# Reciprocal roots of RMS norms: a power on GpSimd with an addition on VectorE, in place of Ln and Exp on ScalarE

## The chip, the cores and the metric

The kernel runs on all eight cores of one Trainium2 chip. Each core computes one of the eight samples of the batch, and no core waits for another. The metric is the device time of the slowest core, in microseconds (us). Executions of a kernel mostly agree within a few tenths of a per cent, but some fall into a slower state, in which the four cores of one die show a lower granted TensorE clock and the time is longer by some per cent, whatever the kernel. Such runs are called slow below.

## The reference

The model is a trunk of two layers. Each layer has three sub-layers (a SwiGLU feed-forward block, a mixer, a second feed-forward block), and each sub-layer begins with an RMS norm over 1024 channels. A last norm follows, so there are seven norms over 2048 tokens. The code is shortened.

```python
D_MODEL = 1024; BATCH = 8; SEQ = 2048; EPS = 1e-6

def rmsnorm(x, g):
    y = x * lax.rsqrt(jnp.mean(x * x, axis=-1, keepdims=True) + EPS)
    return y * g

def modulate(x, g, mod):
    shift, scale, gate = jnp.split(mod, 3, axis=-1)
    return rmsnorm(x, g) * (1.0 + scale) + shift, gate

# per layer:  x += 1/2 * gate * SwiGLU_1(h);  x += gate * Mixer(h);  x += 1/2 * gate * SwiGLU_2(h)
#             with h, gate = modulate(x, ...) before each;  at the end: rmsnorm(x, final_g)
```

The change concerns one thing alone: how `rsqrt(mean + EPS)` is computed.

## The kernel before

Activations lie transposed. `X` has the 128 channels of a chunk in the partitions, eight chunks, and 2048 tokens along the free dimension, worked on in four tiles of `TT = 512` tokens. The sum of squares over channels therefore runs across partitions, and TensorE forms it: ScalarE squares the chunks, and eight matmuls with a 128x128 matrix of ones add them. Every one of the 128 rows of the result in PSUM (a 128x512 tile) holds the same sum, so it can be multiplied into `X` as it is. ScalarE turns it into the reciprocal root as exp(-0.5 ln(x)), and VectorE multiplies.

```python
def ones_pair(t, c, b):                       # sum over channels, broadcast to all partitions
    for x in (c, c + 1):
        n = 12 * (t // 2) + x
        add("pe", I("matmul", PS[b][:], ONES[:], TB[:, n, :].bitcast(BF16), start=(x == 0), stop=(x == NC - 1)), ...)

def rstd_ops(ts, bs):                         # the part that changes
    for t, b in zip(ts, bs):
        rs, k = rs_of(t)
        add("act", I("activation", out=rs, in_=PS[b][:], func=AF.Ln, scale=1.0 / D, bias=EPSB[:, 0:1]),
            reads=[("ps", b), "EPSB"], writes=k)
        BK.give(b)
    for t in ts:
        rs, k = rs_of(t)
        add("act", I("activation", out=rs, in_=rs, func=AF.Exp, scale=-0.5), reads=k, writes=k)

# in apply_units: the multiply that waits for rs
add("dve", I("tensor_tensor", out=role.hbuf[:, c:c + 2, tsl(t)], in0=X[:, c:c + 2, tsl(t)],
             in1=rs.unsqueeze(1).broadcast_to([128, 2, TT]), op=ALU.mult), ...)
# ... (cut)
```

`add(engine, instruction, reads, writes)` appends to a list per engine. Each engine executes its list in order and waits at an instruction until what it reads and writes is free. So an instruction that waits holds up all later ones of its engine. GpSimd, otherwise nearly idle, issues the DMAs that load the weights and convert them from fp32 to fp16 (`SLIN<-wp`, `SLOUT<-wp` in the profile), in the same in-order list. And the program has 24 places with a 128x512 reciprocal root: six stages (the prologue, the entry of the first mixer, the second feed-forward block, the second layer's first block, the stage of the pooling mixer, and the final norm), each with four token tiles. Two more, of 128x8, belong to the pooling mixer.

## Time and profile before

The median was 2119.45 us of three runs (2114.96 to 2266.61; the run of 2266.61 us was slow).

| before | value |
|---|---|
| time, median | 2119.45 us |
| span of the profiled slowest core (core 2) | 2134.3 us |
| TensorE (PE) busy | 95% |
| VectorE (DVE) / ScalarE (ACT) / GpSimd (POOL) busy | 64% / 33% / 5% |
| mean granted clock per core | 0.971 to 0.989 |

In this profiled execution cores 2 and 3 were mildly slowed (clock 0.971 and 0.972, spans 2134.3 and 2132.5 us); the other six took 2104.6 to 2111.5 us.

Lines from the page of the kernel before: busy time of each engine with its share of the span and its instructions, then the busy tenths in 40 equal slices of the span (9 is 90% or more), then the chain of waits that ended last by engine.

```profile
PE 2037.6 (95%) x9611; PEld 918.9 (43%) x9634; DVE 1361.1 (64%) x2573; ACT 709.9 (33%) x1068; POOL 117.1 (5%) x227
...
PE   6999999999999989999998899999998899999996
...
POOL 0000000001210000000000000100100100000000
PEclk9888999999999999999999999999999999999998
...
PE 82%; DVE 8%; issue 4%; ACT 3%; DMA 3%; DVEq 0%; SPq 0%; ACTq 0%; POOL 0%; POOLq 0%
```

The kernel is bound by TensorE from end to end. Nothing that only makes ScalarE faster can win more than TensorE's idle 5%.

Groups of instructions of the kernel before on ScalarE, the five that the change removes or thins out. The columns are line, engine, operation, names, shapes and count, then busy us and mean ns of one, then the engine's idle time just before and what ended it. All lines read L253 because one helper records every instruction.

```profile
L253 ACT ACT_TABLE_LOAD x38 | 48.8, 1283 | 52.0 <-PE ps L253 48.0 <-DMA SM<-small 3.6
...
L253 ACT ACTIVATE TSUM<-ps,EPSB 128x512 f32<-128x512 f32 x20 | 13.5, 687 | 6.7 <-PE ps L253 6.6
...
L253 ACT ACTIVATE TSUM<-TSUM 128x512 f32<-128x512 f32 x20 | 12.1, 627 | 1.1
...
L253 ACT ACTIVATE TP<-ps,EPSB 128x512 f32<-128x512 f32 x4 | 2.7, 687 | 0.0
L253 ACT ACTIVATE TP<-TP 128x512 f32<-128x512 f32 x4 | 2.5, 630 | 0.4
```

`ps,EPSB` are the Ln, the two groups without EPSB the Exp: 30.8 us in all. The table loads come from alternating Ln and Exp with the activations of the blocks. The Trainium skill, ScalarE: Activation LUTs, section "What ACT_TABLE_LOAD costs", gives about 1283 ns for the load, and this trace has 1283.

The only powers in the kernel before, from the same view for GpSimd:

```profile
L253 POOL TENSOR_TENSOR STAT<-STAT,MHALF 128x1 f32<-128x1 f32 x16 | 9.4, 590 | 2.4
```

They have one column each.

Longest waits of TensorE on other engines in the kernel before, with the wait of GpSimd's weight loads for a free slot above them (columns: total us, times, longest us):

```profile
POOL SLIN L253 <- PE ps L253: 1156.5, 91, 64.5
...
PE ps L253 <- DVE ps L253: 23.8, 17, 3.1
...
PE ps L253 <- DVE TSUM L253: 13.4, 7, 7.8
...
PE ps L253 <- ACT TSUM L253: 9.4, 10, 2.7
```

TensorE hardly waits. GpSimd waits most of the time, chiefly for a weight slot that TensorE has to finish with first. It loads ahead by a few slots and no further.

### The profile page before, as it was taken

How to read it: one execution, taken by the hardware profiler on the slowest of the kernel's cores; microseconds unless marked ns; L12 is line 12 of the kernel's file. 1: busy time of each engine (PE TensorE's matmuls, PEld its weight loads, DVE VectorE, ACT ScalarE, POOL GpSimd, SP SyncE). 2: the span in 40 equal slices, each digit the busy share in tenths (PEclk: the TensorE clock that was granted, in tenths of full speed). 3: DMA queues.
4: the chain of work that ended last, by engine and by line, in shares of the span. 5: the costliest groups of instructions: out<-in, count | busy, mean ns of one | idle time of the engine just before them, and what ended most of it. 6: DMA issues, size and time to landing. Idle time of an engine off the chain costs nothing.

```text
span 2134.3 us, 29994 instructions; the slowest of 8 cores (2104.6 to 2134.3 us)
## 1 busy us (share of the span) xinstructions
PE 2037.6 (95%) x9611; PEld 918.9 (43%) x9634; DVE 1361.1 (64%) x2573; ACT 709.9 (33%) x1068; POOL 117.1 (5%) x227
## 2 busy tenths in 40 slices
PE   6999999999999989999998899999998899999996
PEld 1344444444644434444443344444454444444442
DVE  1556677747777777677665876555657675555555
ACT  2531131334422453032125531230354653240342
POOL 0000000001210000000000000100100100000000
PEclk9888999999999999999999999999999999999998
DMA  9535283515046125355352253230543414231313
GB/s 272 143 65 119 90 167 105 127 27 100 10 99 142 27 50 133 93 139 142 98 109 41 46 113 99 45 67 13 90 77 51 80 31 70 39 70 20 65 47 116
DMA packets 73575, 183.45 MB, mean 86 GB/s; under 512 B 7248, under 2 KB 11472, under 8 KB 72528
## 3 DMA queue, kind: packets, MB, share of 16 engines
q0 software_dynamic: 28416, 92.29, 25.4%
q1 hardware_dynamic: 45008, 89.27, 12.8%
q8 instruction: 81, 1.33, 0.3%
q14 instruction: 70, 0.57, 0.1%
HBM read 257.02 MB, written 8.39 MB: 124 GB/s over the span
## 4 chain that ended last, share of the span: by engine, by line
PE 82%; DVE 8%; issue 4%; ACT 3%; DMA 3%; DVEq 0%; SPq 0%; ACTq 0%; POOL 0%; POOLq 0%
PE ps L253 82%; DVE H L253 2%; DVE TP L253 2%; DVE X L253 2%; DMA ACTB<-wm 1%; DMA SLIN<-wp 1%; ACT TP L253 1%; DVE ACTB L253 1%; ACT TSUM L253 1%; DVE TSUM L253 1%; ACT L253 1%; DVE ps L253 1%; DVE WMOD L253 1%; DMA WMOD<-wmod 1%; DVE SLIN L253 0%
## 5 line engine op out<-in xcount | busy, mean ns | idle before, releaser
L253 PE MATMUL ps<-H,SLIN 128*128 128x512 f16 x2240 | 544.9, 386 | 20.8 <-DVE ps L253 15.7
L253 PE MATMUL ps<-TSUM,SLIN 128*128 128x512 f16 x2016 | 506.0, 383 | 22.8 <-DVE TSUM L253 10.7
L253 PE MATMUL ps<-ACTB,SLOUT 128*128 128x512 f16 x2368 | 524.5, 382 | 0.0
L253 DVE SCALAR_TENSOR_TENSOR X<-ps,GH,X 128x512 f32<-128x512 f32 x448 | 332.7, 749 | 235.3 <-PE ps L253 233.9
L253 ACT ACTIVATE TP<-ps 128x512 f32<-128x512 f32 x568 | 336.2, 596 | 387.0 <-PE ps L253 313.5
L253 PEld LDWEIGHTS ps<-ACTB,SLOUT 128*128 128x128 f16 x2368 | 232.7, 98 | 283.7 <-issue 20.9
L253 PEld LDWEIGHTS ps<-H,SLIN 128*128 128x128 f16 x2240 | 219.2, 99 | 296.5 <-issue 63.3
L253 ACT ACTIVATE ps<-ps 128x512 f32<-128x512 f32 x168 | 97.8, 582 | 733.0 <-PE ps L253 670.4
L253 PEld LDWEIGHTS ps<-TSUM,SLIN 128*128 128x128 f16 x2016 | 194.1, 98 | 270.0 <-issue 62.4
L253 PE MATMUL ps<-H,SLOUT 128*128 128x512 f16 x1216 | 280.3, 391 | 1.9 <-DVE H L253 1.6
L253 PEld LDWEIGHTS ps<-H,SLOUT 128*128 128x128 f16 x1216 | 121.2, 100 | 155.5 <-issue 41.2
L253 PE MATMUL ps<-ACTB,SLIN 128*128 128x512 f16 x704 | 171.8, 383 | 8.1 <-DVE ps L253 8.1
L253 DVE TENSOR_TENSOR ACTB<-TP 128x512 f16<-128x512 f32 x140 | 96.8, 691 | 116.5 <-ACT TP L253 113.9
L253 DVE TENSOR_TENSOR ACTB<-TP,ps 128x512 f16<-128x512 f32 x156 | 106.9, 687 | 96.2 <-PE ps L253 90.8
L253 DVE TENSOR_TENSOR SLIN<-SLIN 128x512 f16<-128x512 f16 x404 | 162.3, 418 | 4.3 <-DMA SLIN<-wp 4.2
L253 DVE SCALAR_TENSOR_TENSOR WMOD<-WMOD,CB 128x512 f32<-128x512 f32 x240 | 162.5, 682 | 1.4 <-DMA WMOD<-wmod 1.2
L253 DVE TENSOR_TENSOR ps<-ps,TP 128x512 f32<-128x512 f32 x168 | 117.3, 698 | 59.0 <-PE ps L253 55.0
L253 DVE TENSOR_TENSOR TP<-ps,TP 128x512 f32<-128x512 f32 x168 | 115.6, 688 | 39.4 <-PE ps L253 39.2
L253 POOL DMA_DIRECT2D SLIN<-wp x107 | 57.3, 536 | 1245.3 <-PE ps L253 1156.5
L253 ACT ACTIVATE TSUM<-X 128x1024 bf16<-128x1024 f32 (+1 forms) x88 | 95.8, 1127 | 70.6 <-DVE X L253 44.4
L253 PEld LDWEIGHTS ps<-ACTB,SLIN 128*128 128x128 f16 x704 | 67.9, 98 | 88.8 <-issue 13.3
L253 DVE TENSOR_TENSOR H<-TP 128x512 f16<-128x512 f32 x44 | 30.5, 692 | 59.3 <-ACT TP L253 59.0
(95 smaller groups left out, 841.6 us busy)
## 6 DMA issues: line engine op xcount, KB each, us to landing
WMOD<-wmod SPq DMA_DIRECT2D x240, 256.0 KB, 3.3
SLIN<-wp POOLq DMA_DIRECT2D x107, 512.0 KB, 6.0
SLOUT<-wp POOLq DMA_DIRECT2D x60, 512.0 KB, 9.1
X<-xT SPq DMA_DIRECT2D x8, 1024.0 KB, 33.0
outT<-X SPq DMA_DIRECT2D x16, 512.0 KB, 3.1
H<-wm SPq DMA_DIRECT2D x4, 1024.0 KB, 11.7
H<-X POOLq DMA_DIRECT2D x8, 512.0 KB, 4.6
ACTB<-wm SPq DMA_DIRECT2D x3, 1024.0 KB, 23.7
```

Source lines behind the costliest of these rows:

```text
L253: return lambda E: getattr(E, name)(*a, **k)
```

## The change

The intent is to take work and table loads off ScalarE, and to use GpSimd, which was 5% busy. VectorE adds epsilon while it reads the sum from PSUM, since, as the Trainium skill says in Trainium Kernel Development and Optimization, section "Key Constraints", GpSimd cannot access PSUM. GpSimd then raises the tile to the power -0.5. The division by 1024 moves into the matrix of ones.

```diff
+    def pool_rstd(out, ps, rd, wr, n):
+        add("dve", I("tensor_scalar", out=out, in0=ps, scalar1=EPS, scalar2=None, op0=ALU.add), reads=rd, writes=wr)
+        add("pool", I("tensor_tensor", out=out, in0=out, in1=MHALF[:, 0:1].broadcast_to([128, n]), op=ALU.pow),
+            reads=["MHALF"] + wr, writes=wr)
+
     def rstd_ops(ts, bs):
         for t, b in zip(ts, bs):
             rs, k = rs_of(t)
-            add("act", I("activation", out=rs, in_=PS[b][:], func=AF.Ln, scale=1.0 / D, bias=EPSB[:, 0:1]),
-                reads=[("ps", b), "EPSB"], writes=k)
+            pool_rstd(rs, PS[b][:], [("ps", b)], k, TT)
             BK.give(b)
-        for t in ts:
-            rs, k = rs_of(t)
-            add("act", I("activation", out=rs, in_=rs, func=AF.Exp, scale=-0.5), reads=k, writes=k)
# ... (the same in the prologue, st_rstd, and for the two 128x8 tiles of the pooling mixer)
-    add("dve", I("memset", ONES[:], 1.0), writes=["ONES"])
+    add("dve", I("memset", ONES[:], 1.0 / D), writes=["ONES"])
```

More of the change, by code (lines that the diff above doesn't have):

```diff
@@ L1267, in pool_units @@
         R = STAT[:, p, 0:8]
-        V = STAT[:, p, 8:16]
-        add("act", I("activation", out=V, in_=PS[b][:, 0:8], func=AF.Ln, scale=1.0 / D, bias=EPSB[:, 0:1]),
-            reads=[("ps", b), "EPSB"], writes=[("ST", p, 0), ("ST", p, 1), ("ST", p, 2), ("ST", p, 3)])
-        add("act", I("activation", out=R, in_=V, func=AF.Exp, scale=-0.5), reads=[("ST", p, 0)], writes=[("R", p)])
+        pool_rstd(R, PS[b][:, 0:8], [("ps", b)], [("ST", p, 0), ("ST", p, 1), ("ST", p, 2), ("ST", p, 3), ("R", p)], 8)
         BK.give(b)
@@ L1462, in st_rstd @@
         rs = 4 + t % 2
-        add("act", I("activation", out=TP[:, rs, 0:TT], in_=PS[b][:], func=AF.Ln, scale=1.0 / D, bias=EPSB[:, 0:1]),
-            reads=[("ps", b), "EPSB"], writes=[("TP", rs)])
-        add("act", I("activation", out=TP[:, rs, 0:TT], in_=TP[:, rs, 0:TT], func=AF.Exp, scale=-0.5),
-            reads=[("TP", rs)], writes=[("TP", rs)])
+        pool_rstd(TP[:, rs, 0:TT], PS[b][:], [("ps", b)], [("TP", rs)], TT)
         return rs
```

## The prediction

> **What bounds the kernel.** The page gives PE 2037.6 us busy of 2134.3 (95%), VectorE 64%, ScalarE 33%, GpSimd 5%; the chain of waits is 82% PE. Only about 97 us of PE idleness can be won, some 30 of them before the first weights land. Ln and Exp matter only where a norm's scale is waited for.
>
> **What goes.** By the groups of instructions: 24 Ln (687 ns) and 24 Exp (about 630 ns) on 128x512, two small pairs, and most of the 38 table loads (1283 ns each), since Ln/Exp alternate with Silu and Gelu: about 75 us of ScalarE, which has much idle time. On the chain, table loads are 0.6% (13 us), and waits around Ln and Exp about as much. Ceiling of the gain: 20 to 25 us.
>
> **What comes.** 24 VectorE adds out of PSUM (estimate 0.6 us each, between the 546 ns of a 128x512 fp32 tensor_scalar and the 690 ns of a tensor_tensor reading PSUM), and 24 GpSimd powers of 128x512. Both engines run in order: a late power holds the normalising multiply at the head of VectorE's queue, behind it the evictions that PE waits for; and it delays weight DMAs that GpSimd issues.
>
> **The cost of the power** is the crux; none of that size is in the trace. A 128x1 power takes 568 ns, a 128x1 tensor_scalar 222 ns undisturbed: 350 ns more for one vector per core. The Trainium skill, GPSIMD Engine Reference, section 3.1 says that a longer loop body runs at about 3 operations per cycle, and section 7 gives 4 cycles for a dependent fp32 operation. Some 300 cycles for one dependent pass would be 75 operations; perfectly overlapped, 25 cycles a column, for 512 columns 10 us (an estimate from those figures). Unoverlapped it is far more; if the 350 ns is mostly fixed cost, 2 to 4 us. The skill's page SBUF — State Buffer, section "SBUF: two separate sides", says that a GpSimd operation and a VectorE operation with two SBUF inputs exclude each other for a whole instruction; the trace agrees: a 222 ns tensor_scalar took 1031 ns beside such a 1.2 us multiply.
>
> **On the path.** Old latency from last ones-matmul to multiply: about 2.7 us (load, Ln, Exp), 1.5 us at the very end. New: 0.7 us plus the power. With 10 us, 8 us more at each of 24 places; the prologue's four, the pairs inside the feed-forward groups, the mixer's, and the last two, in series with the end, are exposed nearly whole; those amid output projections are partly covered by free PSUM banks. About half exposed: +100 us, less 20 us gained. With a 2 to 3 us power the result is 0 to 1% faster; with 20 us, over 10% slower.
>
> **Prediction.** 2200 us, 8 in 10 between 2090 and 2440. Faster by over 2%: 7%; within 2%: 33%; slower by over 2%: 60%.
>
> **What would show it.** The group of the 128x512 power: mean about 10 us, total 240 us, GpSimd busy near 16%. VectorE idle before normalising multiplies, released by GpSimd, 100 us or more in the list of waits. ScalarE busy near 635 us with under 8 table loads: right whatever the power costs. In windows of the prologue (30 to 110 us) and the end (2040 us on) the delay per power is plainest. Granted clock unchanged.
>
> **What would make it wrong.** A power below 4 us: the removed loads win slightly. A power not overlapped at all: beyond my range. GpSimd's hold on the shared port stopping VectorE more than the latency does.

## The result, and the profile after

| | before, same chip | after |
|---|---|---|
| median (all runs) | 2119.55 us of 4 (2114.96 to 2266.61) | 4133.64 us of 4 (4049.90 to 4308.27) |
| fast runs | | 4049.90 and 4077.29 us |
| ratio of fast runs | | 1.919 (95%: 1.902 to 1.935) |

The changed kernel takes almost twice as long. Ratios in this document are the mean time of one kernel's fast runs over that of the other's of the same rounds, so not quite the ratio of the medians. The profiled run was a fast one: all eight cores lie between 4032.6 and 4048.3 us.

The same lines of the page for the kernel after (core 6):

```profile
PE 2052.5 (51%) x9634; PEld 922.1 (23%) x9634; DVE 1380.9 (34%) x2599; ACT 635.1 (16%) x981; POOL 2086.4 (52%) x253
...
PE   3111699803229311189980313999904409991120
...
POOL 4888300296770788810029686010295690008888
PEclk7556899956659755599995656999956759995565
...
PE 41%; POOL 35%; issue 14%; DVE 5%; DMA 3%; POOLq 2%; ACT 1%; SPq 0%; DVEq 0%; ACTq 0%
```

PE is busy for nearly the same number of microseconds, spread over twice the span. Read the rows of PE and POOL against each other: where POOL shows 8 or 9, PE shows 0 to 2, and where POOL shows 0, PE shows 9. The two engines take turns, in six blocks, one for each stage with norms. The row of the clock sinks only in those blocks.

Groups of the kernel after: the powers on GpSimd and the table loads on ScalarE (the second fence).

```profile
L253 POOL TENSOR_TENSOR TSUM<-TSUM,MHALF 128x512 f32<-128x512 f32 x20 | 1638.6, 81933 | 316.3 <-DVE TSUM L253 316.3
L253 POOL TENSOR_TENSOR TP<-TP,MHALF 128x512 f32<-128x512 f32 x4 | 327.7, 81931 | 50.2 <-DVE TP L253 50.2
...
L253 POOL TENSOR_TENSOR STAT<-STAT,MHALF 128x1 f32<-128x1 f32 x16 | 9.4, 589 | 2.4
...
L253 POOL TENSOR_TENSOR STAT<-STAT,MHALF 128x8 f32<-128x8 f32 x2 | 3.3, 1666 | 1.6 <-DVE STAT L253 1.6
```

```profile
L253 ACT ACT_TABLE_LOAD x3 | 3.8, 1283 | 9.0 <-PE ps L253 4.9 <-DMA SM<-small 4.1
```

One power of 128x512 takes 81.93 us, not the predicted 10. The 24 of them take 1638.6 + 327.7 = 1966 us. The time grew by 4049.9 - 2119.6 = 1930 us. So 98% of the power time has become time of the kernel. The three widths give the cost per column: (1666 - 589) / 7 = 154 ns between one and eight columns, (81,931 - 1666) / 504 = 159 ns between 8 and 512. The cost is close to linear from the first column on.

Waits of the kernel after, those of VectorE and TensorE that were absent or small before:

```profile
DVE H L253 <- POOL TSUM L253: 807.3, 10, 81.6
...
DVE X L253 <- POOL TSUM L253: 328.9, 4, 82.3
PE ps L253 <- DVE SLIN L253: 324.9, 7, 81.0
...
DVE ACTB L253 <- POOL TSUM L253: 307.3, 4, 80.8
...
PE ps L253 <- ACT TSUM L253: 248.0, 6, 83.2
PE ps L253 <- DMA SLIN<-wp: 245.6, 10, 84.9
PE ps L253 <- DVE H L253: 231.0, 5, 78.2
```

VectorE's waits are each about one power long: 82 us at most. TensorE's waits have two kinds of releaser. Some are engines that had been waiting for the normalised data (ACT TSUM, DVE H). Others are weights, the DMA `SLIN<-wp`: a weight load behind a power in GpSimd's one in-order list is not issued until the power ends. VectorE's `SLIN`, a combination of two weight slots, looks like the second kind, but the timeline of VectorE and TensorE puts nearly all of it with the first:

```profile
876.38 0.41 DVE L253 TENSOR_TENSOR SLIN<-SLIN 128x512 f16<-128x512 f16 x1
...
876.94 3.47 PE L253 MATMUL ps<-TSUM,SLIN 128*128 128x512 f16 x8 [80.96 <-DVE SLIN L253]
```

The combination had no wait of its own. It stood behind a normalising multiply on VectorE that had waited 80.99 us for a power and began at 873.86 us (its line is shown further below). TensorE stopped for more than 10 us 23 times, 1838.6 us in all. Traced back in this way, 20 of the stops (1600.7 us) end behind such a multiply, among them the four long ones under `DVE SLIN`; 3 (237.9 us) end with a weight load that GpSimd issued behind a power.

The first power in time order, in the timeline of the kernel after (start us, duration us, instruction, and in brackets the idle time before it with its releaser); the lines are those of VectorE, GpSimd and TensorE:

```profile
40.33 0.69 DVE L253 TENSOR_SCALAR TP<-ps 128x512 f32<-128x512 f32 x1 [38.84 <-PE ps L253]
...
50.20 0.53 POOL L253 DMA_DIRECT2D SLOUT<-wp  x1 [8.85 <-DMA X<-xT]
54.25 1.59 POOL L253 DMA_DIRECT2D SLIN<-wp  x3 [3.52 <-DMA X<-xT]
55.83 81.97 POOL L253 TENSOR_TENSOR TP<-TP,MHALF 128x512 f32<-128x512 f32 x1
...
137.97 4.63 DVE L253 TENSOR_TENSOR TSUM<-X,TP 128x1024 f32<-128x1024 f32 x4 [96.95 <-POOL TP L253]
...
143.34 1.84 PE L253 MATMUL ps<-WMOD,TP 4*128 4x4 f32 x8 [96.17 <-DVE TP L253]
```

VectorE's addition is done at 41.0 us. The power starts only at 55.83, because weight loads that wait for the input's DMAs stand ahead of it in GpSimd's list. Then it runs for 82 us. VectorE's multiply waits 97 us, and TensorE, whose next operand VectorE delivers behind that multiply, 96 us. In the kernel before the Ln and Exp of this tile ended at 43.4 us.

To see where the time was lost, I took the start of each of TensorE's 9634 weight loads (the order is the same in both kernels) and subtracted the start of the same one in the kernel before. The table shows how much that delay grew over each stage, worked out from the traces. It is compared with core 0 of the kernel before, whose span was 2104.6 us at a clock of 0.989. Each column is one core, mostly the fastest of its run; undisturbed cores of one run differ by 10 us and more (2123.0 to 2134.0 us in e2, 4032.6 to 4048.3 after), so entries of a few us say little by themselves. Between the stages it changes by 4 us or less in every column, and the sum of all parts is the last row.

| stage (4 tiles each) | after, core 4 | e1, core 4 | e2, core 4 | e3, core 0 | e9, core 1 |
|---|---|---|---|---|---|
| prologue | 333.7 | 48.0 | 14.6 | 12.3 | -1.4 |
| entry of the first mixer | 319.5 | 35.9 | 4.0 | 5.7 | 1.6 |
| second feed-forward block | 325.4 | 39.7 | 1.8 | 0.0 | 2.8 |
| second layer, first block | 316.4 | 30.4 | -1.8 | -2.7 | -1.8 |
| pooling mixer | 310.9 | 24.2 | 2.8 | 2.1 | 2.3 |
| final norm | 323.1 | 38.8 | 0.1 | -2.5 | 1.0 |
| whole span | 1928.0 | 214.6 | 18.5 | 13.0 | 1.3 |

Four powers are 4 x 81.93 = 327.7 us. In the changed kernel each stage loses 95 to 102% of that. Nowhere does the pipeline around the norm hide a power. (e1 to e9 are experiments, below.)

TensorE's lower mean clock, 0.754, is a consequence and not a cause. Its matmuls take the same time on average (383 to 386 ns in the groups `ps<-H,SLIN` and `ps<-TSUM,SLIN` of both kernels), and it is busy for 15 us more. What a stop costs is seen where TensorE resumes after one, in the timeline of the kernel after:

```profile
961.96 3.57 PE L253 MATMUL ps<-H,SLIN 128*128 128x512 f16 x8 [76.82 <-DMA SLIN<-wp]
...
968.87 1.89 PE L253 MATMUL ps<-H,SLIN 128*128 128x512 f16 x8
```

The first eight matmuls took 3.57 us, eight of the same kind 7 us later 1.89. That agrees with the Trainium skill, TensorE: Matmul & The Clock Gate, section "What's actually happening", where the array falls to half its clock after about 3.4 us of idleness and stays there until it has been busy for as long. Some two microseconds after each of the 23 long stops, about 40 us, do not explain 1930.

### The profile page after: what moved, and what is told of

Read it like the earlier page. It is cut to its first block, busy times and chain, and to the rows that moved or that the text cites. A ratio compares the mean times of both kernels' runs of the same rounds, so it can differ in the third digit from the quotient of the medians.

```text
span 4048.3 us, 30043 instructions; the slowest of 8 cores (4032.6 to 4048.3 us)
## 1 busy us (share of the span) xinstructions
PE 2052.5 (51%) x9634; PEld 922.1 (23%) x9634; DVE 1380.9 (34%) x2599; ACT 635.1 (16%) x981; POOL 2086.4 (52%) x253
## 4 chain that ended last, share of the span: by engine, by line
PE 41%; POOL 35%; issue 14%; DVE 5%; DMA 3%; POOLq 2%; ACT 1%; SPq 0%; DVEq 0%; ACTq 0%
PE ps L253 41%; POOL TSUM L253 27%; POOL TP L253 8%; POOLq L1601 2%; DMA SLIN<-wp 2%; DVE TP L253 1%; DMA X<-xT 1%; DVE H L253 1%; DVE X L253 1%; DVE TSUM L253 1%; DVE ACTB L253 0%; SPq L253 0%; ACT TP L253 0%; DMA WMOD<-wmod 0%; DVE WMOD L253 0%
## 5 line engine op out<-in xcount | busy, mean ns | idle before, releaser
L253 POOL TENSOR_TENSOR TSUM<-TSUM,MHALF 128x512 f32<-128x512 f32 x20 | 1638.6, 81933 | 316.3 <-DVE TSUM L253 316.3
L253 POOL TENSOR_TENSOR TP<-TP,MHALF 128x512 f32<-128x512 f32 x4 | 327.7, 81931 | 50.2 <-DVE TP L253 50.2
L253 DVE TENSOR_TENSOR H<-X,TSUM 128x1024 f16<-128x1024 f32 x48 | 60.3, 1257 | 807.3 <-POOL TSUM L253 807.3
L253 PE MATMUL ps<-TSUM,ONES 128*128 128x512 bf16 x192 | 57.3, 405 | 324.1 <-ACT TSUM L253 248.0
L253 ACT ACTIVATE H<-H,MODT,AS 128x512 f16<-128x512 f16 x48 | 39.0, 813 | 1065.1 <-DVE H L253 1065.0
L253 POOL DMA_DIRECT2D SLOUT<-wp x60 | 32.5, 544 | 314.6 <-PE ps L253 265.4
```

What stands on the lines that cost most here:

```text
L253: return lambda E: getattr(E, name)(*a, **k)
```

## The experiments

The theory after the result (A): the power costs about 159 ns for each column, and its whole latency is exposed, because VectorE and GpSimd work in order. Rivals: (B) it is not the latency of the result but GpSimd's late weight loads; (C) the running power holds the memory port that it shares with VectorE, and VectorE's work stands still. Besides, the claims of my prediction about exposure and about the gain on ScalarE had to be measured by themselves. Several kernels below give a wrong result: they raise only some of the columns or partitions to the power. The other elements hold min(variance + epsilon, 1), so that nothing overflows; the sizes and the order of everything else stay, except for the edits of order that are named.

### Cost by width: 64 columns, 8 columns, and 16 of the 128 partitions

The edit, with `m = min(n, 64)`, `min(n, 8)` in e2; e3b keeps 512 columns and 16 partitions:

```diff
-        add("dve", I("tensor_scalar", out=out, in0=ps, scalar1=EPS, scalar2=None, op0=ALU.add), reads=rd, writes=wr)
-        add("pool", I("tensor_tensor", out=out, in0=out, in1=MHALF[:, 0:1].broadcast_to([128, n]), op=ALU.pow),
+        add("dve", I("tensor_scalar", out=out, in0=ps, scalar1=EPS, scalar2=1.0, op0=ALU.add, op1=ALU.min), reads=rd, writes=wr)
+        m = min(n, 64)
+        add("pool", I("tensor_tensor", out=out[0:128, 0:m], in0=out[0:128, 0:m], in1=MHALF[0:128, 0:1].broadcast_to([128, m]), op=ALU.pow),
```

Expected of 64 columns:

> Wrong result on purpose: the power runs on the first 64 of 512 columns; the rest of each scale is min(variance + epsilon, 1). From 568 ns at 1 column, 1666 ns at 8 and 81.93 us at 512 the power should take about 10.6 us, which is the 10 us of my forecast. Theory A (a power is exposed at 98% of its length, as in the changed kernel): 4050 - 24 x 71.3 x 0.98 = about 2370 us. Theory B (my forecast's step: about half of a 10 us power hides behind free PSUM banks and other work): about 2200 us. So this run separates the cost of the power from the exposure that I assumed.

Expected of 8 columns:

> Wrong result on purpose: the power runs on 8 of 512 columns (1.67 us each, as the 128x8 group of the changed kernel shows), everything else of the change stays. If the length of the power is the whole loss, the time falls back to before, less what Ln, Exp and 35 of 38 table loads were worth: 2090 to 2120 us, with about 14 us lost in the prologue, where the first power stands in the queue behind weight loads until 55.8 us. If the added VectorE operation or the extra hop costs by itself, 2150 us or more.

Expected of 16 partitions with all 512 columns:

> Wrong result on purpose: the power on 512 columns but on 16 of 128 partitions, an eighth of the elements. If the power's time goes with columns, each still takes about 82 us and the run about 4050 us; if it goes with elements, about 10.6 us and about 2390 us. (All 128 partitions hold the same 512 values, so this tells whether dropping the repeated rows would help.)

Measured, the groups of powers of the three kernels (all wrong), one fence each:

```profile
L253 POOL TENSOR_TENSOR TSUM<-TSUM,MHALF 128x64 f32<-128x64 f32 x20 | 210.7, 10537 | 322.0 <-DVE TSUM L253 322.0
```

```profile
L253 POOL TENSOR_TENSOR TSUM<-TSUM,MHALF 128x8 f32<-128x8 f32 x20 | 32.9, 1649 | 313.3 <-DVE TSUM L253 313.3
```

```profile
L253 POOL TENSOR_TENSOR TSUM<-TSUM,MHALF 16x512 f32<-16x512 f32 x20 | 1638.5, 81930 | 316.1 <-DVE TSUM L253 316.1
```

| | power, ns | median us | fast runs, us | ratio to before, 95% |
|---|---|---|---|---|
| 128x512 (the change) | 81,932 | 4133.64 | 4049.90, 4077.29 | 1.919 (1.902 to 1.935) |
| 16x512 (e3b) | 81,930 | one run | 4049.06 | not timed in rounds |
| 128x64 (e1) | 10,537 | 2395.95 | 2363.61, 2382.89 | 1.125 (1.112 to 1.138) |
| 128x8 (e2) | 1649 | 2139.00 | 2137.28 to 2164.48 | 1.008 (1.000 to 1.015) |

The runs of before beside e1 to e4 had a median of 2138.19 us (11 runs); its fast ones lay between 2115.04 and 2138.91.

The cost goes with the columns, not with the elements: an eighth of the partitions saves nothing. This fits what the Trainium skill says in GPSIMD Engine Reference, section "1. Specifications", that each of GpSimd's cores owns 16 partitions and is 16 numbers wide. A column of the tile is then one vector on each, however many cores have work. No dependence on the values shows: the 20 powers of the changed kernel lie between 81,906 and 81,962 ns.

e1 is the most instructive for the prediction, because it has exactly the cost that I had assumed: 10.5 us a power. Had half of it been exposed, as I predicted, it would have lost about 80 us. On core 4, undisturbed in both runs, it lost 214.6 us where e2 lost 18.5. The difference, 196.1 us, stands against 24 x (10.54 - 1.65) = 213 us by which its powers are longer than those of e2: 92% exposed. Even against the whole 24 x 10.54 = 253 us of power it is 78%. The ratio of the fast runs, 1.125, says about 265 us; but two of its four runs were slow, and of the profiled one two cores had a clock of 0.924 against 0.943 of core 4, so I rely on that core. The failing step is thus twofold: with the right cost of the power I would still have been wrong by more than 100 us. e2 missed its expectation of 2090 to 2120 us: with 2139 us it is not faster than before, and stays below the 2150 us that an added cost by itself was to show. What it lost is followed up below.

### Is it GpSimd at all, or the power? A multiply of 512 columns

In e3 `ALU.pow` becomes `ALU.mult` on all 512 columns (wrong). All instructions, waits and queues stay.

> Wrong result on purpose: a multiply by -0.5 in place of the power, on all 512 columns of GpSimd. If the power itself is what is slow, each takes 1 to 2 us and the run lies within 20 us of the run with 8 columns of power; if a wide two-input operation on GpSimd is slow whatever it computes, each stays above 10 us and the run above 2300 us.

The group of the multiply:

```profile
L253 POOL TENSOR_TENSOR TSUM<-TSUM,MHALF 128x512 f32<-128x512 f32 x20 | 20.6, 1034 | 315.2 <-DVE TSUM L253 315.2
```

The median was 2129.14 us, the ratio 0.9995 (0.993 to 1.006). The detour over two engines costs nothing that these runs resolve; only the operation does. A multiply takes 1034 / 512 = 2.0 ns a column, the power 159 ns: 79 times as much. The Trainium skill, GPSIMD Engine Reference, section 3.1, measures about 2.6 cycles an element for a two-input operation at 1.2 GHz, by my estimate 2.2 ns; the 2.0 ns here are near that. In the same cycles a power is 159.3 x 1.2 = 191 cycles a column, an estimate from that page's clock.

The trace is finer than the ratio here: the table by stages shows e3 losing 12.3 us in the prologue and 5.7 at the first mixer, and winning a little elsewhere.

### Occupying GpSimd while nobody waits for the result

e4 is the kernel before, with its Ln and Exp and a right result. At each of the 24 places GpSimd also executes nine powers of 56 columns into a scratch tile that nobody reads. A one-column copy on ScalarE releases them.

```diff
+    def dummy(b):
+        i = ndum[0]
+        ndum[0] += 1
+        add("act", I("activation", out=TRG[:, i:i + 1], in_=PS[b][:, 0:1], func=AF.Copy), reads=[("ps", b)], writes=[("TRG", i)])
+        for _ in range(9):
+            add("pool", I("tensor_tensor", out=DUM, in0=EPSB[:, 0:1].broadcast_to([128, 56]), in1=MHALF[:, 0:1].broadcast_to([128, 56]), op=ALU.pow),
+                reads=["MHALF", "EPSB", ("TRG", i)], writes=["DUM"])
```

> The kernel before, with Ln and Exp kept, and at each of 24 norms nine powers of 56 columns on GpSimd that nobody waits for (about 9.3 us each, 82 to 84 us together), started by a small ScalarE copy of the same bank. Right results. Theory A (the loss is VectorE waiting for the power's result): under 2250 us. Theory B (the loss is also GpSimd being occupied: its weight loads are issued up to 82 us late): 2500 us or more, with PE waiting for SLIN and SLOUT loads. Theory C (a running power shuts VectorE operations with two SBUF inputs out): those operations, 0.42 us and 1.2 us long, would start only when a power ends; in the changed kernel's trace they already seem to run beside one, so I expect not.

Measured: two runs, 3830.84 us fast and 3923.97 slow. Its powers and its longest wait of TensorE:

```profile
L253 POOL TENSOR_TENSOR DUM<-EPSB,MHALF 128x56 f16<-128x56 f32 x216 | 2009.5, 9303 | 198.7 <-ACT DUM L253 168.8 <-POOL DUM L253 1.2
```

```profile
PE ps L253 <- DMA SLIN<-wp: 1376.4, 14, 278.6
```

With nobody waiting for a power, the kernel still loses about 1710 us, 85% of the 2009.5 us of power. The reason stands in the wait: TensorE waits for weights, once for 278.6 us, because their DMAs are issued from the queue that the powers fill. (VectorE also waited 150 us for small GpSimd operations that stood behind the powers.) So theory A as I put it, latency of the result alone, is not the whole of it. Theory B is no rival that has to be ruled out: GpSimd's queue alone would be enough to lose most of the time.

In the changed kernel itself it is mostly the other path that ends a wait: by the count above, 1600.7 of TensorE's 1838.6 us of long stops end with the late result and 237.9 with late weights. That tells which path came last, not what would be left if one of them were removed. That the late result alone would cost as much is not shown: I found no kernel that makes only the result late without occupying some engine for 82 us.

### Does a running power block VectorE's port?

The Trainium skill, SBUF — State Buffer, section "SBUF: two separate sides", says that a VectorE operation with two SBUF inputs and a GpSimd operation that reads SBUF exclude each other for the whole instruction of the one that came first. My prediction rested on it. The traces of before and after answer this without a further run. First, the timeline of the kernel after, in which the GpSimd line holds two powers that follow each other; the second of them lasts until 955.66 us:

```profile
791.82 163.84 POOL L253 TENSOR_TENSOR TSUM<-TSUM,MHALF 128x512 f32<-128x512 f32 x2 [4.57 <-DVE TSUM L253]
...
873.86 2.00 DVE L253 TENSOR_TENSOR H<-X,TSUM 128x1024 f16<-128x1024 f32 x1 [80.99 <-POOL TSUM L253]
...
877.98 1.21 DVE L253 TENSOR_TENSOR H<-X,TSUM 128x1024 f16<-128x1024 f32 x1
```

The multiply with two SBUF inputs at 877.98, in the midst of the second power, took 1.21 us. So did all 12 such multiplies that ran within a power (1.21 to 1.23 us). In the kernel before the same multiply took 1.22 at 553.87 us, with GpSimd idle. Of those that met a power, only the four that began just as it started took longer, 2.00 us. The other direction does hold, in the timeline of the kernel before (its first line is the multiply just named):

```profile
553.87 1.22 DVE L253 TENSOR_TENSOR H<-X,TSUM 128x1024 f16<-128x1024 f32 x1
...
558.48 1.03 POOL L253 TENSOR_SCALAR STAT<-STAT 128x1 f32<-128x1 f32 x1 [13.69 <-DVE STAT L253]
...
560.48 0.22 POOL L253 TENSOR_SCALAR STAT<-STAT 128x1 f32<-128x1 f32 x1 [0.25 <-DVE STAT L253]
```

The GpSimd operation at 558.48 began during a VectorE multiply (558.24, 1.19 us) and took 1.03 us; without one, 0.22. So theory C falls for these powers: once running, they do not keep VectorE off. e4 shows the same: during its powers such a multiply, at 66.47 us, took 1.23 us.

### The loss without a power: order in GpSimd's queue

e2 lost 14.6 us in the prologue and 4.0 at the first mixer, although its powers are short. The timeline of e2 shows the first (GpSimd and TensorE, core 7):

```profile
56.40 1.59 POOL L253 DMA_DIRECT2D SLIN<-wp  x3 [8.78 <-DMA X<-xT]
57.99 1.69 POOL L253 TENSOR_TENSOR TP<-TP,MHALF 128x8 f32<-128x8 f32 x1
...
65.21 1.84 PE L253 MATMUL ps<-WMOD,TP 4*128 4x4 f32 x8 [18.49 <-DVE TP L253]
```

The short power stands behind three weight loads that wait for the input. TensorE waits 18.5 us for what follows it, where it waited 1.4 us in the kernel before. At the mixer it is the reverse: weight loads stand behind powers that are not ready. Two edits undo that: the first tile keeps Ln and Exp on ScalarE, and three weight loads of the mixer are recorded earlier.

```diff
+        if t > 0:
+            pool_rstd(TP[:, rs, 0:TT], PS[b][:], [("ps", b)], [("TP", rs)], TT)
+            return rs
+        add("act", I("activation", out=TP[:, rs, 0:TT], in_=PS[b][:], func=AF.Ln, bias=EPSB[:, 0:1]), ...)
+        add("act", I("activation", out=TP[:, rs, 0:TT], in_=TP[:, rs, 0:TT], func=AF.Exp, scale=-0.5), ...)
# and, in the output loop of the first feed-forward block:
+            if (l, s, t) == (0, 0, 2) and n_sub_run > 1:
+                for q, piece in enumerate((("abv", 0), ("abv", 1), ("abu", 0))):
+                    load_piece(piece, q)
```

My first version, e6, and its control e7 (the kernel before with the early loads alone) recorded the loads a step too early, where the last group of the block still reads one of the slots. e7 therefore has an error of 0.023 that I had not intended.

> Wrong result on purpose, as the run with 8 columns, with two edits of order alone: the first tile's scale stays with Ln and Exp on ScalarE (so no power stands behind the gated weight loads), and the mixer's first three weight loads are issued ahead of the power of the third tile. Against the 8-column run, weight load by weight load on TensorE, I read 16 us lost in the prologue and 4 to 8 us at the entry of the mixer, nothing elsewhere. If GpSimd's in-order queue is the cause of both, those steps go and the time falls by about 20 us to 2100 to 2118 us, level with before or 0.5% faster. If VectorE's added operation or the hop to GpSimd is the cause, it stays above 2125 us.

> A control: the kernel before, with only the mixer's first three weight loads issued earlier. Right results. In the kernel before they waited for nothing that TensorE missed, so same within 0.3%; if it is faster by more, that part of any gain of the next run belongs to the order of loads and not to the power.

Measured: e6 2126.09 us, ratio 1.0039 (1.0025 to 1.0052); e7 2123.42 us, 1.0025 (1.0012 to 1.0038). By its own expectation e6 fell on the side of the rival (above 2125 us). But the misplaced loads cost about 5 us by themselves, so it proves little either way. With the loads in the right place, e9 is e2 with both edits, and e10 the control, which gives the right result:

> Wrong result on purpose: the 8-column run with the two edits of order, the early loads now in their right place. Theory A (GpSimd's in-order queue made the 16 us and 4 to 8 us steps): 2105 to 2120 us, level with before. Then taking 48 ScalarE passes and 27 or more table loads away is worth under 0.5%. If the run is over 1% faster than before, the removed ScalarE work was worth what I forecast (20 us).

> Control: the kernel before with only the early mixer loads, in the right place. Right results, same time as before within 0.3%.

Measured: e9's fast runs took 2117.29, 2117.48, 2118.84 and 2137.01 us (two more were slow), ratio 1.0030 (0.9987 to 1.0073). e10 had a median of 2117.58, ratio 0.9998 (0.9981 to 1.0014); before, 2118.40. In the table by stages e9 no longer loses in the prologue (-1.4 instead of 14.6) nor, beyond 2 us, at the mixer. Over the cores, each against core 0 of the kernel before, the prologue's loss falls from 12 to 16 us (the six cores of e2 at a clock of 0.978 or more) to none (all eight of e9), the mixer's from 5 to 12 us to 2 to 5 us. So the order of the queue was the cause of the first step and of the greater part of the second; the rest of the second stays open.

e9 has a second use. It is free of Ln and Exp but for one tile, has 5 table loads instead of 38, and its powers are nearly free. It is about the best that the idea of the change could do, and it is level with before. The gain of 20 to 25 us that I had put into the sum does not appear. (e9 still has the added VectorE passes and the hop to GpSimd, so this is a net figure; what the removed ScalarE work is worth by itself was not measured.)

### A correct version with a short power

Since the power costs by column and all 128 rows of the sum are equal, one can form the sums as 128x4 (tokens in the partitions), raise four columns, and spread the result afterwards. e5 and e8 do this at the 20 places after the prologue: 32 one-column matmuls give the sums, GpSimd computes a 128x4 power and writes it onto a diagonal, a matmul with ones broadcasts it, and ScalarE copies it out. The prologue keeps Ln and Exp.

```diff
+    def rstd_pow(t, b):
+        pool_rstd(STC[:, t, :], PS[b][:, 0:4], [("ps", b)], [("STC", t)], 4)
+        BK.give(b)
+    def rstd_diag(t, dg, k):
+        add("pool", I("affine_select", out=dg.rearrange("p (n j) -> p n j", n=4), in_=STC[:, t, :].unsqueeze(2).broadcast_to([128, 4, 128]),
+                      pattern=[[0, 4], [1, 128]], compare_op=ALU.is_equal, fill=0.0, base=0, channel_multiplier=-1), ...)
+    def rstd_bc(dg, k, rs, rk):
+        b = BK.take()
+        add("pe", I("matmul", PS[b][:], ONES[:], dg, start=True, stop=True), reads=["ONES", k], writes=[("ps", b)])
+        add("act", I("activation", out=rs, in_=PS[b][:], func=AF.Copy, scale=float(D)), reads=[("ps", b)], writes=rk)
# ... (the sums as 128x4, in fp16)
```

> A version with right results that takes the power where it is cheap: the sums of squares land as 128 tokens by 4 columns (32 narrow matmuls in place of 8 wide ones), the power runs on 4 columns (about 1.05 us from 590 ns and 154 ns a column), GpSimd spreads the 4 columns on a diagonal (about 0.6 us), one matmul with a constant matrix brings them back to 128 x 512, ScalarE copies out of PSUM; prologue on ScalarE and the three early loads as in the run beside it. Theory A (only the length of the power and the queue order made the change slow): 2095 to 2120 us, level with before or up to 1% faster, with under 12 table loads. If the longer path of five hops is exposed at each of 20 norms by 2 us: 2150 us.

e5 took 2135.88 us, ratio 1.0082 (1.0069 to 1.0095), outside the 2095 to 2120 us expected. It has the misplaced loads of e6 and the same unintended error of 0.023, and TensorE waited 27.2 us for the diagonal because the broadcasting matmul stood too early in its list. e8 mends both: the matmul comes four steps later.

> The version with the power on 4 columns again, with two faults of mine mended. The early weight loads overwrote a slot that one last group still read (error 0.0235 in the two runs that had it and right arithmetic, and 4.7 us of waiting): they now come after that group. And the broadcasting matmul stood too early in TensorE's order (27 us of waiting for GpSimd): it now comes four steps of the background work later. Right results. Theory A (these two and the length of the power were all): 2136 less 5 less most of 27 us, so 2100 to 2118 us, level with before or up to 0.9% faster. If the norm's longer path only moves the wait elsewhere: 2120 us or more, and waits on GpSimd turn up as waits on VectorE.

e8 gives the right result. Its median was 2114.22 us against 2118.40, and its ratio 0.9998 (0.9965 to 1.0032). Its power and TensorE's wait for the diagonal, from two views of e8:

```profile
L253 POOL TENSOR_TENSOR STC<-STC,MHALF 128x4 f32<-128x4 f32 x20 | 20.5, 1027 | 370.0 <-DVE STC L253 370.0
```

```profile
PE ps L253 <- POOL TSUM L253: 7.4, 7, 3.1
```

So the changed kernel's loss of 1930 us can be undone with the power still on GpSimd, by making it 4 columns wide. But it brings the kernel back to where it was, and no version that I ran is faster than the kernel before by more than the fast runs resolve. A small gain of e8 is possible: on dies whose cores all had a clock above 0.977 the median core took 2105 us (40 cores), against 2110 us before (68 cores), 0.2% less.

## Why the prediction was wrong

The direction was right, and slower by over 2% was the likeliest case given. The size was far off: 2200 us predicted, 2440 as the upper end, and 4050 us measured in fast runs.

**The step that failed first: "perfectly overlapped, 25 cycles a column, for 512 columns 10 us".** Measured: 81.93 us, 159 ns or some 191 cycles a column, eight times the forecast. I had 350 ns for one column more than a simple operation, put some 300 cycles of it down to the calculation, and shrank these twelvefold by an assumed overlap of the columns, out of the figures for tight loops of the Trainium skill (GPSIMD Engine Reference, sections 3.1 and 7). Nothing in the trace of before said that the columns overlap. It held powers of one column only, and one width has no slope. The same trace gave a bound for no overlap: 512 x 0.35 = 179 us. The truth, 82, lies between 10 and 179; how much of the 350 ns is fixed cost and how much the columns do overlap stays open. An honest range would have reached far beyond 2440. The text did say "A power not overlapped at all: beyond my range"; it should have given that case weight.

**The second: "About half exposed".** Measured: 98% of the power time in the changed kernel, 78 to 92% with powers of 10.5 us (e1). I had counted on free PSUM banks. But VectorE stands at the multiply, and what TensorE needs next stands behind it (20 of the 23 long stops); and GpSimd's list holds the next weights, by itself enough to stop TensorE (e4).

**The third: "less 20 us gained".** Measured: nothing, net of what the change adds. e9, with 5 table loads of 38 left and powers of 1.65 us, is at 1.003 (0.999 to 1.007). TensorE's waits on `ACT TSUM`, the name under which Exp stands beside the squares, hardly shrink without it (12.3 us before on core 0, 10.8 in e9 on core 1), and TensorE's idle time between matmuls stays the same (81 to 94 us over the cores of before, 83 to 94 in e9).

With my own formula the parts can be sized. At 24 places, new latency is 0.7 + power, old latency 2.7. With 81.93 us a power, half of it exposed and 20 us gained, it gives 24 x 79.9 / 2 - 20 = 939 us of loss instead of some 80: in this sum the cost of the power accounts for about 860 us of the error. Full exposure adds 24 x 79.9 / 2 = 959, and the missing gain 20. That makes 1918 us; 1930 was measured. The sum fits, but its terms were sized after the result, so it is a description and no proof.

**"Granted clock unchanged"** was wrong as a number (0.754), since TensorE idles half the time and the clock sinks in the slices where it does; the mean durations of the matmuls did not change. **"GpSimd's hold on the shared port"** was named as a risk; the running powers did not hold VectorE up.

**What was right:** ScalarE busy near 635 us (635.1) with under 8 table loads (3); the main new wait is VectorE before its normalising multiplies, released by GpSimd; the cost of the power is the crux; in the prologue the delay is plainest, since 333.7 of 1928 us are lost there.

## What to carry to other kernels

A profile that shows an operation only at its smallest size does not tell its cost per element; before an operation is moved to an engine that the program has never used for it at size, time it at two widths, and make the range wide enough for both "all overlapped" and "nothing overlapped". An engine that is 5% busy may still issue the loads that everything depends on: on an in-order engine, a long operation delays all that stands behind it, whether or not anyone waits for its result. Removing work from an engine that is not the bottleneck gained nothing net here: in e9, 33 table loads and 46 activations of 128x512 went away, and the time stayed.

## What the Trainium skill lacked or had wrong

- GPSIMD Engine Reference, section 3.1: there is no figure for a power on GpSimd, on this page or another. Measured: 0.57 to 0.59 us for 128x1, 1.03 for 128x4, 1.65 to 1.67 for 128x8, 10.54 for 128x64, 81.93 for 128x512, and the same 81.93 for 16x512. That is 159 ns a column against 2.0 ns for a multiply in the same place. The page's "roughly 3 ops/cycle" for longer loop bodies did not carry over to a power with the number of operations that I guessed: the estimate was 10 us.
- SBUF — State Buffer, section "SBUF: two separate sides": the exclusion for the whole instruction was not seen from the side of a running power. VectorE multiplies with two SBUF inputs took 1.21 to 1.23 us in the midst of one, as without one; only the four that began at the start of a power took 2.00. In the other direction it was seen (1.03 us instead of 0.22 on GpSimd).
- No page that I read warns that weight DMAs issued by GpSimd stand behind its compute operations. Measured in e4: 1376.4 us of TensorE waiting for weights while GpSimd executed powers whose result nobody used.
